# Turning one attention's operands through DRAM instead of on TensorE, in a two-block transformer kernel

## The chip, the cores and the metric

The kernel runs on one core of a Trainium2 chip. The metric is the device time of one execution in microseconds (us), lower is better. A difference is told as a share of the time before.

## What is computed

Two transformer blocks follow each other on 256 tokens of width 2048, all in f32. The first block:

```python
mod = silu(c) @ w_ada + b_ada
shift_a, scale_a, gate_a, shift_f, scale_f, gate_f = split(mod, 6)
h = rms_norm(x, g_attn_pre) * (1 + scale_a) + shift_a
proj = h @ w_in                     # d_q, d_k, d_v, s_q, s_k, s_v, i_q, i_k, i_w
diff = (softmax(q1 k1^T) - lam * softmax(q2 k2^T)) @ v    # 8 heads, causal
dsa  = attention over the 64 best keys of each query      # 8 heads, one shared key
mixed = concat(rms_norm(diff), dsa) @ w_o
x = x + gate_a * rms_norm(mixed, g_attn_post)
ff = (silu(h2 @ w_gate) * (h2 @ w_up)) @ w_down           # h2: x normed and modulated
x = x + gate_f * rms_norm(ff, g_ffn_post)
```

The second block projects the normed `x` by `w_in_2` (2048 to 19520 columns), has a latent attention (two latents of 512, `qa` and `ck`, each normed and projected up again), a gated convolution of length 3, two output products, a merge and `w_out_2`.

## The kernel before

**Products.** 256 tokens are two tiles of 128 (`t` = 0, 1). Each large product is a `Grp` of up to 512 output columns; it walks over the contraction in chunks of 128 rows (`kc`). Weights are f32; ScalarE (ACT) rounds a weight tile into `wh` and VectorE (DVE) computes the rest `wl` (`pump_split`, L286 and L287), two chunks at a time, and TensorE (PE) multiplies three times for each chunk and token tile: `hi*wh`, `hi*wl`, `lo*wh`. These are the rows `mm` of line L65. The left operand lies transposed, features on partitions, as a pair `hi`, `lo`.

**Order.** The program is written out once, in Python, in the order of a model clock: `run` issues the products one after the other and adds up PE's modelled time in `clock["t"]`; everything else is a generator in `bg` (softmax stages, norms, evictions) that yields how long it wants to be left alone, and `tick` resumes it when the model clock has come that far. So the model decides only in which order each engine's queue is filled; on the chip each queue runs in that order, as fast as its semaphores let it. Where a product needs something that the model has not finished, `require` resumes the generators one after the other with no product between them, and then `keep_warm` (L346) issues 12 dummy 512-column products before the real one.

**Buffers.** 14 slots of 1 MB (`big`, `free`) hold all large tensors. Weights are loaded by SP into a ring of 4 `raw` buffers; `lend(n)` adds up to n of the free slots to the ring (`rawb`).

**The first attention block.** The projection accumulates the columns of `w_in` in SBUF in slices: `accA0`, `accA1` (keys and queries of four difference heads each), `accS` (queries of the sparse attention), `accC`, `accV`. The last 12 chunks of the difference columns come in the order of `D_G`: 1024, 0, 2048 (first half: heads 0 to 3), 1536, 512, 2560 (second half). Merged into these products are those of the modulation rows (`ada`, 1 MB of `w_ada` for four narrow products). `idx_gen` scores and picks the keys, `dsa_gen` is the sparse attention, `diff_gen` the difference attention. Each attention is a `pipe` of stages: scores on PE (`sA`), softmax (`sB`, `sC`), transposed probabilities on PE (`sD`), product with the values (`sE`), norm (`sF`), transposed result (`sG`), which writes `mh0`, `ml0`. `diff_gen` runs two pipes, one for each half: it waits for `dsa`, ropes `accA`, turns four blocks of 128x512 by four PE transposes each (`quad_transpose`, L70), which ACT and DVE copy from PSUM into `kTz` and `dqT`, and starts the pipe of four heads for both token tiles. `w_o` comes in two products: `wo1` (needs the sparse attention, with `ada` rows merged in) and `wo2` (needs the difference attention, through `need=["diff", "ada2"]`).

**Other places.** `row_fin` spreads a modulated gate row over 128 partitions by four f32 products with a column of the identity (`br` and `brt`, L732). `lora_norm` turns a latent by `quad_transpose`; `post_ck1` turns the rope key `kd`; `post_z` turns group 0 of the gated attention.

**The way through DRAM** exists already as `flip_quad` (L558): DVE transposes 32x32 blocks into `scr`, four DMAs on SP write them to a DRAM tile in runs of 128 bytes, so that it lies transposed, and one DMA reads it back. It is used for the feed-forward activations and for most groups of the second block.

## Time and profile before

| | before |
|---|---|
| median of 3 runs | 2349.62 us (2348.67 to 2350.85) |
| profiled execution | 2349.08 us, its span 2347.4 us |
| PE busy | 2295.9 us, 98% of the span |
| DVE, ACT, POOL busy | 1331.7, 1066.2, 96.8 us |
| chain of work that ended last | 73% of the span on PE, 70% of it in `mm` of L65 |
| DMA | 528.60 MB, mean 225 GB/s |

Busy time of an engine is the union of its instructions' durations. Consecutive products overlap in the records: a 512-column `mm` lasts 0.39 us but the next starts 0.23 us later, so what a product costs is read from the distance of the starts.

### The profile page before, as it was taken

To read this page: it belongs to the slowest core of one execution; us is meant where nothing else is said; L and a number is where in the kernel's file an instruction comes from. 1 tells how busy PE (TensorE), PEld (TensorE's weight loads), DVE (VectorE), ACT (ScalarE), POOL (GpSimd) and SP (SyncE) were. 2 spreads that over 40 slices of the span, in tenths; PEclk is the share of its full clock that TensorE was granted. 3 is DMA by queue.
4 is the path that set the end of the run, shared out by engine and by line. 5 is a ranking of instruction groups with operands and counts; after the bars stand their busy time and mean duration, and the time that the engine had idled before them with its cause. 6 is when DMAs were issued, how large, how long until landed. Compare 5 with 4: busy or idle time off the path is not lost.

```text
span 2347.4 us, 27890 instructions
## 1 busy us (share of the span) xinstructions
PE 2295.9 (98%) x10876; PEld 1824.8 (78%) x10876; DVE 1331.7 (57%) x1752; ACT 1066.2 (45%) x1495; POOL 96.8 (4%) x117
## 2 busy tenths in 40 slices
PE   7899999999999999999998999999999999999998
PEld 5666666677887888888887888888888988888887
DVE  3646755556765455554556655656645654664665
ACT  4434344546444444434444644444445544444443
POOL 1311011010000000000001000000000000000000
PEclk9999999999999999999999999999999999999999
DMA  9987888868885566655764667776665553686773
GB/s 308 329 317 242 310 306 303 316 212 291 261 293 200 195 209 209 211 197 190 210 201 154 222 201 213 222 223 211 202 199 162 168 173 126 185 259 200 222 228 126
DMA packets 348500, 528.60 MB, mean 225 GB/s; under 512 B 98664, under 2 KB 142864, under 8 KB 339280
## 3 DMA queue, kind: packets, MB, share of 16 engines
q1 hardware_dynamic: 346272, 518.18, 67.6%
q0 software_dynamic: 1872, 8.58, 1.1%
q8 instruction: 85, 1.39, 0.2%
q14 instruction: 47, 0.39, 0.0%
q10 hardware_dynamic: 224, 0.07, 0.0%
HBM read 511.57 MB, written 15.20 MB: 224 GB/s over the span
## 4 chain that ended last, share of the span: by engine, by line
PE 73%; DVE 2%; ACT 1%; DMA 1%; issue 1%; SPq 0%; POOL 0%; DVEq 0%; POOLq 0%; ACTq 0%
PE mm L65 70%; PE sc L65 1%; PE tp L65 1%; DMA fm<-flip 1%; PE tp L70 1%; DVE wl L287 0%; SPq L566 0%; PE tpb L70 0%; ACT wh L286 0%; DVE xr L1175 0%; ACT h3h L1183 0%; DVE h3l L1186 0%; POOL rstd L513 0%; ACT junk L1198 0%; DVE ot L1740 0%
## 5 line engine op out<-in xcount | busy, mean ns | idle before, releaser
L287 DVE TENSOR_TENSOR wl<-raw,wh 128x1024 fp32r<-128x1024 f32 (+3 forms) x723 | 869.2, 1210 | 741.1 <-ACT wh L286 735.0
L286 ACT ACTIVATE wh<-raw 128x1024 fp32r<-128x1024 f32 (+3 forms) x723 | 745.7, 1039 | 736.4 <-PE mm L65 710.9
L65 PE MATMUL mm<-wh,h3h 128*128 128x512 f32 (+1 forms) x992 | 385.5, 389 | 1.7 <-ACT h3h L1183 1.2
L65 PE MATMUL mm<-wl,h3h 128*128 128x512 f32 (+1 forms) x992 | 380.9, 384 | 1.2 <-DVE wl L287 1.2
L65 PE MATMUL mm<-wh,h3l 128*128 128x512 f32 (+1 forms) x992 | 380.9, 384 | 0.0
L65 PE MATMUL mm<-wl,h2h 128*128 128x512 f32 x704 | 274.5, 390 | 0.9 <-DVE wl L287 0.9
L65 PE MATMUL mm<-wh,h2h 128*128 128x512 f32 x704 | 274.8, 390 | 0.0
L65 PE MATMUL mm<-wh,h2l 128*128 128x512 f32 x704 | 274.4, 390 | 0.0
L65 PEld LDWEIGHTS mm<-wh,h3h 128*128 128x128 f32 x992 | 186.8, 188 | 38.9 <-ACT h3h L1183 1.6
L65 PEld LDWEIGHTS mm<-wh,h3l 128*128 128x128 f32 x992 | 186.5, 188 | 37.3 <-DVE h3l L1186 0.4
L65 PEld LDWEIGHTS mm<-wl,h3h 128*128 128x128 f32 x992 | 186.8, 188 | 36.4 <-DVE wl L287 1.7
L65 PE MATMUL mm<-wh,h1h 128*128 128x512 f32 (+2 forms) x384 | 153.9, 401 | 3.9 <-ACT wh L286 3.1
L65 PEld LDWEIGHTS mm<-wl,h2h 128*128 128x128 f32 x704 | 132.6, 188 | 28.5 <-DVE wl L287 1.2
L65 PEld LDWEIGHTS mm<-wh,h2h 128*128 128x128 f32 x704 | 132.5, 188 | 28.3 <-issue 0.8
L65 PEld LDWEIGHTS mm<-wh,h2l 128*128 128x128 f32 x704 | 132.4, 188 | 27.3
L65 PE MATMUL mm<-wl,h1h 128*128 128x512 f32 (+2 forms) x384 | 142.7, 372 | 8.0 <-DVE wl L287 8.0
L65 PE MATMUL mm<-wh,h1l 128*128 128x512 f32 (+2 forms) x384 | 142.1, 370 | 1.9 <-DVE h1l L647 1.9
L65 PE MATMUL mm<-wh,acth 128*128 128x512 f32 x352 | 139.3, 396 | 0.0
L65 PE MATMUL mm<-wh,actl 128*128 128x512 f32 x352 | 137.1, 390 | 0.0
L65 PE MATMUL mm<-wl,acth 128*128 128x512 f32 x352 | 136.9, 389 | 0.0
L65 PEld LDWEIGHTS mm<-wh,h1h 128*128 128x128 f32 x384 | 72.7, 189 | 56.2 <-issue 25.9
L65 PEld LDWEIGHTS mm<-wl,h1h 128*128 128x128 f32 x384 | 73.0, 190 | 21.3 <-DVE wl L287 10.9
(413 smaller groups left out, 2753.1 us busy)
## 6 DMA issues: line engine op xcount, KB each, us to landing
raw<-in_w_in_dram SPq DMA_DIRECT2D x134, 1024.0 KB, 5.3
raw<-in_w_ada_dram SPq DMA_DIRECT2D x47, 1024.0 KB, 5.2
raw<-in_w_gate_dram SPq DMA_DIRECT2D x44, 1024.0 KB, 5.2
raw<-in_w_up_dram SPq DMA_DIRECT2D x44, 1024.0 KB, 5.5
raw<-in_w_down_dram SPq DMA_DIRECT2D x44, 1024.0 KB, 5.1
raw<-in_w_ada_dram SPq DMA_DIRECT2D x36, 512.0 KB, 8.4
rawb<-in_w_ada_dram SPq DMA_DIRECT2D x17, 1024.0 KB, 6.8
raw<-in_w_o_conv_dram SPq DMA_DIRECT2D x16, 1024.0 KB, 5.1
```

What stands on the lines that cost most here:

```text
L65: return nc.tensor.matmul(o, l, r, **kw)
L70: return nc.tensor.transpose(o, i, idn)
L286: A.activation(wh[:, :m, :g.n], src, AF.Copy)
L287: V.tensor_sub(wl[:, :m, :g.n], src, wh[:, :m, :g.n])
```

## The change

Three groups of edits. **First attention:** the operands of both attentions leave `accS` and `accA` through DRAM. `flip_quad` is split into `flip_out` (turn, write) and `flip_in` (read back); `dsa_prep` and the new `diff_out` issue these DMAs on POOL. The destination slots are asked for by `claim`, which waits until slots are free and keeps the ring from taking them. `diff_gen` starts after the last score product of the sparse attention (`dsascores`) instead of after its end, and runs one pipe over all 16 items; `ready` holds the whole pipe in front of an item whose operands have not been read back. **Rows:** `row_fin` writes the four pieces of a gate row to DRAM and reads them back on every partition. **Second block:** the two latents, `kd` and group 0 of `post_z` go through DRAM on SP's queue.

The diff, without its unchanged lines (the list of `diff_gen`'s second half is cut):

```diff
@@ -200 +200 @@
-    lent = {"now": 0, "max": 0}
+    lent = {"now": 0, "max": 0, "claims": 0}
@@ -215 +216 @@
+    def claim(n):
+        lent["claims"] += n
+        while True:
+            while len(slots) < n and reclaim():
+                pass
+            if len(slots) >= n:
+                break
+            yield POLL
+        lent["claims"] -= n
+
@@ -216 +227 @@
+        if it["res"][0] == "big" and len(slots) < lent["claims"]:
+            slots.append(it["res"][1])
+            lent["now"] -= 1
+            return
@@ -246 +260 @@
-                if lent["now"] < lent["max"] and len(slots) > 0:
+                if lent["now"] < lent["max"] and len(slots) > lent["claims"]:
@@ -366 +380 @@
-    def pipe(items, stages, offs, every):
+    def pipe(items, stages, offs, every, ready=None):
@@ -372 +387 @@
+            if ready is not None and j == 0:
+                while not ready(items[i]):
+                    yield POLL
@@ -558 +575 @@
-    def flip_quad(src, dst=None):
+    def flip_out(src, n=512, wait=2.0, scr=None, eng=nc.sync):
@@ -561 +578 @@
-        scr = wtile(tag="PT", bufs=2, name="scr")
-        V.transpose(scr, src)
-        yield 2.0
+        if scr is None:
+            scr = wtile(tag="PT", bufs=2, name="scr")
+        v = scr[:, :n]
+        V.transpose(v if len(src.shape) == 2 else v.rearrange("p (h d) -> p h d", h=src.shape[1]), src)
+        yield wait
@@ -565 +584 @@
-            d = bass.AP(tensor=dr.tensor, offset=dr.offset + 32 * i, ap=[[P, 32], [32 * P, 16], [1, 32]])
-            nc.sync.dma_start(d, scr[32 * i:32 * i + 32].rearrange("p (b r) -> p b r", r=32))
+            d = bass.AP(tensor=dr.tensor, offset=dr.offset + 32 * i, ap=[[P, 32], [32 * P, n // 32], [1, 32]])
+            eng.dma_start(d, scr[32 * i:32 * i + 32, :n].rearrange("p (b r) -> p b r", r=32))
@@ -567 +587 @@
+        return dr
+
+    def flip_in(dr, dst, b0=0, step=4, p0=0, n=P, eng=nc.sync):
+        s = bass.AP(tensor=dr.tensor, offset=dr.offset + b0 * 32 * P + p0 * P,
+                    ap=[[P, n], [step * 32 * P, dst.shape[1]], [1, P]])
+        eng.dma_start(dst, s)
+
+    def flip_quad(src, dst=None):
+        dr = yield from flip_out(src)
@@ -570 +598 @@
-        s = bass.AP(tensor=dr.tensor, offset=dr.offset, ap=[[P, P], [P * P, 4], [1, P]])
-        nc.sync.dma_start(dst, s)
+        flip_in(dr, dst)
@@ -730 +757 @@
-            for j in range(4):
-                pb = tp_bank()
-                T.matmul(pb, ident[:, 32 * j:32 * j + 1].to_broadcast([P, P]), br, start=True, stop=True)
-                A.activation(hid[name][:, 512 * j:512 * (j + 1)], pb, AF.Copy)
-                yield
+            line = drp.tile([4, 512], F32, name=f"line{name}")
+            G.dma_start(line, br[0:P:32, :])
+            yield 10.0
+            G.dma_start(hid[name], bass.AP(tensor=line.tensor, offset=line.offset, ap=[[0, P], [1, D]]))
+            yield 10.0
@@ -872 +900 @@
+        mark("picks")
@@ -902 +930 @@
-        sqT = big("sqT")
-        hid["sqT"] = sqT
+        drs = {}
@@ -909 +936 @@
-                pb = quad_transpose(acc["S"][:, t, 512 * q:512 * (q + 1)])
-                A.activation(sqT[:, 4 * q:4 * q + 4, t * P:(t + 1) * P], pb, AF.Copy)
-                yield 2.07
+                drs[t, q] = yield from flip_out(acc["S"][:, t, 512 * q:512 * (q + 1)], eng=G)
@@ -915 +941 @@
+        while not done("picks"):
+            yield POLL
+        yield from claim(1)
+        sqT = big("sqT")
+        hid["sqT"] = sqT
+        for t in range(2):
+            for q in range(2):
+                flip_in(drs[t, q], sqT[:, 4 * q:4 * q + 4, t * P:(t + 1) * P], eng=G)
+        yield FLIP
@@ -936 +971 @@
+            if it == (1, 3):
+                mark("dsascores")
@@ -980 +1017 @@
+    kTz = {}
+
+    def diff_out(q):
+        while not done(f"win{512 * q}_d.1", f"win{1024 + 512 * q}_d.1"):
+            yield POLL
+        src = acc["A", q]
+        for t in range(2):
+            rope(src[:, t].rearrange("p s (n d) -> p (s n) d", d=64)[:, :, 0:16], 16, t)
+        yield 4.0
+        drs = {}
+        for t in range(2):
+            for s in range(2):
+                drs[t, s] = yield from flip_out(src[:, t, 1 - s, :], 512, 3.0, wtile(name="scr"), G)
+        free(f"accA{q}")
+        while not done("dsa" if q else "dsascores"):
+            yield POLL
+        yield from claim(1 if q else 2)
+        if q == 0:
+            hid["dqT"] = big("dqT")
+        dqT = hid["dqT"]
+        kTz[q] = big(f"kTz{q}", (P, 4, 2, 256))
+        G.memset(kTz[q], 0.0)
+        yield 4.0
+        for t in range(2):
+            tok = slice(t * P, (t + 1) * P)
+            flip_in(drs[t, 0], kTz[q][0:64, :, 0, tok], 0, 4, 0, 64, G)
+            flip_in(drs[t, 0], kTz[q][64:128, :, 1, tok], 0, 4, 64, 64, G)
+            flip_in(drs[t, 1], dqT[:, 4 * q:4 * q + 4, tok], eng=G)
+        yield FLIP
+
@@ -982 +1048 @@
-        while not done("dsa"):
+        while not done("dsascores", "diffin0"):
@@ -984 +1050 @@
-        kTz = {}
-        dqT = big("dqT")
+        dqT = hid["dqT"]
@@ -1059 +1125 @@
+            mh, ml = mhml
@@ -1065 +1131 @@
-        for q in range(2):
-            kTz[q] = big(f"kTz{q}", (P, 4, 2, 256))
-            G.memset(kTz[q], 0.0)
...
-                pb = quad_transpose(src[:, t, 0, :])
-                A.activation(dqT[:, 4 * q:4 * q + 4, t * P:(t + 1) * P], pb, AF.Copy)
...
+        mhml = []
+
+        def ready(it):
+            q = it[1] // 4
+            if not done(f"diffin{q}", f"win{2048 + 512 * q}_d.1"):
+                return False
+            return bool(mhml)
+
+        def outputs():
+            while not done("dsa"):
@@ -1088 +1142 @@
-            yield from pipe([(t, h) for t in range(2) for h in range(4 * q, 4 * q + 4)],
-                            [sA, sB, sC, sD, sE, sF, sG],
-                            [0.0, 1.12, 4.01, 9.5, 12.09, 13.2, 19.98], 2.64)
-            free(f"kTz{q}")
+            yield from claim(2)
+            hid["mh0"], hid["ml0"] = big("mh0", dt=R32), big("ml0", dt=R32)
+            mhml.extend((hid["mh0"], hid["ml0"]))
+
+        spawn(outputs())
+        yield from pipe([(t, h) for q in range(2) for t in range(2) for h in range(4 * q, 4 * q + 4)],
+                        [sA, sB, sC, sD, sE, sF, sG],
+                        [0.0, 1.12, 4.01, 9.5, 12.09, 13.2, 19.98], 2.64, ready)
+        free("kTz0", "kTz1")
@@ -1110 +1170 @@
+    def start_out():
+        for q in range(2):
+            spawn(diff_out(q), f"diffin{q}")
+
@@ -1132 +1196 @@
+    sd.insert(0, call(start_out))
+    sd.insert(1, call(lambda: lend(2)))
@@ -1367 +1432 @@
-        yield
-        pb = quad_transpose(x)
-        m = wtile(name="lm")
-        m3 = m.rearrange("p (c q) -> p c q", q=P)
-        V.tensor_mul(m3, pb, col2[:, goff:goff + 4][:, :, None].to_broadcast([P, 4, P]))
+        go = flip_quad(x)
+        d = next(go)
+        mark(f"turned{goff}.{t}")
+        yield d
+        m3 = yield from go
+        V.tensor_mul(m3, m3, col2[:, goff:goff + 4][:, :, None].to_broadcast([P, 4, P]))
@@ -1387 +1453 @@
-        require([f"r3.{t}", "qa.0", "qa.1"], "ck0")
+        require([f"r3.{t}", "turned0.0", "turned0.1"], "ck0")
@@ -1402 +1468 @@
-        yield
-        pb = quad_transpose(kd[:, :P])
-        A.activation(zk[0:64, 0, t * P:(t + 1) * P], pb[0:64, 0, :], AF.Copy)
-        A.activation(zk[64:128, 1, t * P:(t + 1) * P], pb[64:128, 0, :], AF.Copy)
+        dr = yield from flip_out(kd[:, :P], P)
+        flip_in(dr, zk[0:64, 0:1, t * P:(t + 1) * P], 0, 4, 0, 64)
+        flip_in(dr, zk[64:128, 1:2, t * P:(t + 1) * P], 0, 4, 64, 64)
+        yield FLIP
@@ -1654 +1720 @@
-            if g:
-                m3 = yield from flip_quad(d)
-            else:
-                yield
-                m3 = quad_transpose(d)
+            m3 = yield from flip_quad(d)
```

How the rows of the queues move, at three places. In these rows `tp` is a PSUM bank for transposes and small products, `osb` the attention's output before it is turned, `p` the probabilities, `pt` the same transposed, `mh1`/`ml1` and `mh0`/`ml0` the operands of `wo1` and `wo2`, `adasb` the copy of a finished modulation row.

**PE, where `wo1` ends and `wo2` begins.** Before, the last row of the difference attention is the `osb` row here, and six products of `wo1`, an `ada` row of four products, six more products and another `ada` row lie between it and `wo2`:

```order
L65 MATMUL mm_4094<-wh_4030,mh1_2607 128x512
L65 MATMUL mm_4094<-wl_4031,mh1_2607 128x512
L65 MATMUL mm_4094<-wh_4030,ml1_2608 128x512
L70 MATMUL tp_4159<-ident_99,osb_4092 128x128 x4
L65 MATMUL mm_4076<-wh_4070,mh1_2607 128x512
L65 MATMUL mm_4076<-wl_4071,mh1_2607 128x512
L65 MATMUL mm_4076<-wh_4070,ml1_2608 128x512
```

After the change, at the end of `wo1`:

```order
L65 MATMUL mm_3965<-wh_4028,ml1_2650 128x512
L65 MATMUL ada_3556<-raw_3861,csil_117 32x512 x4
L70 MATMUL tp_4168<-ident_99,p_4044 128x128 x2
L70 MATMUL tp_4172<-ident_99,osb_4095 128x128 x4
L70 MATMUL tp_4179<-ident_99,p_4081 128x128 x2
L70 MATMUL tp_4183<-ident_99,adasb_4155 128x128 x4
L65 MATMUL tp_4191<-accV_267,pt_4097 128x128 x4
L65 MATMUL tp_4191<-accV_267,pt_4167 128x128 x4
L70 MATMUL tp_4214<-ident_99,osb_4200 128x128 x4
L360 LDWEIGHTS negi_104
L360 MATMUL mm_4221<-caus_106,negi_104 128x512
```

The end of the difference attention now stands behind the last product of `wo1` with no large product between its rows, and the 12 dummy products of `keep_warm` (now L360) follow before `wo2`. The last score product of the difference attention stands 78 large products ahead of `wo2` before and 18 after the change. The first half's scores hardly move; the second half's first score product stands 66 products later than before, and ahead of it the pipe of all 16 items issues nothing on PE for 156 large products.

**ACT, at the same place.** Before, from the last copies of the difference attention on:

```order
L1022 ACTIVATE pt<-tp 128x256
L286 ACTIVATE wh<-raw 128x1024
L1037 ACTIVATE osb<-tp 128x512
L1046 ACTIVATE sq<-osb 128x512
L286 ACTIVATE wh<-raw 128x1024 x2
L1061 ACTIVATE mh_3151<-tp,gdiff 128x4x128
```

After the change:

```order
L1223 ACTIVATE mo_3523<-mm 128x512
L726 ACTIVATE adasb<-ada 128x512
L300 ACTIVATE wh<-rawb 128x1024 x2
L1087 ACTIVATE pt<-tp 128x256
L1127 ACTIVATE mh_3151<-tp,gdiff 128x4x128
L1087 ACTIVATE pt<-tp 128x256
L1102 ACTIVATE osb<-tp 128x512
L1111 ACTIVATE sq<-osb 128x512
L1127 ACTIVATE mh_3151<-tp,gdiff 128x4x128
```

The copy of the modulation row and two weight splits now stand ahead of the last two `pt` copies.

**POOL, from the first half's end to the second half's scores.** Before:

```order
L800 TENSOR_TENSOR accA_266<-pa,accA_266 128x512
L513 TENSOR_TENSOR rstd<-rstdv,mhalf 128x4
L800 TENSOR_TENSOR accV<-pa,accV 128x512
L513 TENSOR_TENSOR rstd<-rstdv,mhalf 128x4
L1067 MEMSET kTz_3612 128x2048
```

After:

```order
L585 DMA flip_3535<-scr 32x16x32 x4
L760 DMA Ga<-lineGa 128x2048
L585 DMA flip_3632<-scr 32x16x32 x4
L1038 MEMSET kTz_3708 128x2048
L592 DMA kTz_3708<-flip_3317 64x4x128 x2
L592 DMA dqT<-flip_3440 128x4x128
L592 DMA kTz_3708<-flip_3535 64x4x128 x2
L592 DMA dqT<-flip_3632 128x4x128
L530 TENSOR_TENSOR rstd<-rstdv,mhalf 128x4 x3
```

Each half now has 16 writes and 6 reads on POOL's queue, behind the additions into `accA` and around the clearing of `kTz`.

## Rows read from the trace of the kernel before

**Rows 1.** Windows: window, length, busy us of PE, PEld, DVE, ACT, POOL, clock, DMA share, GB/s.

```profile
240.00:480.00 240.00, 240.00 (x1225) 148.82 (x1224) 147.34 (x327) 110.23 (x232) 21.98 (x22) 1.00 0.86 313
```

**Rows 2.** Timeline of PE: start, length, engine, line, operation, out<-in, shape, count.

```profile
411.94 1.02 PE L65 MATMUL tp<-br,ident 128*128 128x512 f32 x2
412.40 0.79 PE L65 MATMUL mm<-wh,mh 128*128 128x512 f32 x1
413.03 0.39 PE L65 MATMUL mm<-wl,mh 128*128 128x512 f32 x1
413.26 0.40 PE L65 MATMUL mm<-wh,ml 128*128 128x512 f32 x1
...
418.97 0.60 PE L70 MATMUL tp<-ident,accA 128*128 128x128 f32 x4
419.32 0.47 PE L65 MATMUL mm<-wh,mh 128*128 128x512 f32 x1
419.64 0.39 PE L65 MATMUL mm<-wl,mh 128*128 128x512 f32 x1
419.86 0.39 PE L65 MATMUL mm<-wh,ml 128*128 128x512 f32 x1
```

**Rows 3.** Groups by line and shape: the dummy products of `keep_warm`; DVE's block transposes.

```profile
L346 PE MATMUL mm<-caus,negi 128*128 128x512 bf16 x24 | 5.5, 379 | 0.0
...
L562 DVE STREAM_TRANSPOSE scr<-act 128x512 f32<-128x512 f32 x16 | 11.4, 711 | 0.6
```

**Rows 4.** Timeline of all engines: the last heads' way from `pt` to `osb`.

```profile
463.04 0.39 ACT L1022 ACTIVATE pt<-tp 128x256 f32<-128x256 f32 x1
...
465.01 1.95 PE L65 MATMUL tp<-accV,pt 128*128 128x128 f32 x16
...
467.00 0.60 ACT L1037 ACTIVATE osb<-tp 128x512 f32<-128x512 f32 x1 [2.63 <-PE tp L65]
467.62 0.63 ACT L1046 ACTIVATE sq<-osb 128x512 f32<-128x512 f32 x1
...
469.26 1.01 POOL L513 TENSOR_TENSOR rstd<-rstdv,mhalf 128x4 f32<-128x4 f32 x1 [10.85 <-DVE rstdv L511]
...
470.30 0.88 DVE L1051 TENSOR_SCALAR osb<-osb,rstd 128x128 f32<-128x128 f32 x4 [1.12 <-POOL rstd L513]
...
472.25 1.06 PE L65 MATMUL ada<-raw,csil 128*32 128x512 f32 x8
472.35 1.06 ACT L286 ACTIVATE wh<-raw 128x1024 fp32r<-128x1024 f32 x1 [2.90 <-PE mm L65]
...
476.10 0.60 PE L70 MATMUL tp<-ident,osb 128*128 128x128 f32 x4
476.73 0.69 ACT L1061 ACTIVATE mh<-tp,gdiff 128x512 fp32r<-128x512 f32 x1 [3.32 <-PE tp L70]
```

**Rows 5.** Timeline of PE at a wait later in the kernel.

```profile
1284.74 1.12 PE L70 MATMUL tp<-ident,xr 128*128 128x128 f32 x4 [4.72 <-DVE xr L1175]
```

**Rows 6.** Windows around that wait.

```profile
1280.00:1284.00 4.00, 0.02 (x1) 0.00 (x0) 2.61 (x7) 2.96 (x7) 0.54 (x1) 0.94 0.00 0
1284.00:1290.00 6.00, 5.26 (x19) 4.57 (x20) 5.04 (x7) 2.33 (x7) 0.00 (x0) 0.50 0.33 98
1290.00:1296.00 6.00, 5.60 (x29) 4.39 (x28) 3.94 (x6) 3.25 (x9) 0.00 (x0) 0.97 0.00 0
```

**Rows 7.** Windows of 50 us without a way through DRAM, and with two.

```profile
800.00:850.00 50.00, 50.00 (x222) 41.40 (x222) 22.59 (x19) 21.38 (x23) 0.00 (x0) 1.00 0.60 190
850.00:900.00 50.00, 50.00 (x222) 41.42 (x221) 25.90 (x25) 22.29 (x23) 0.00 (x0) 1.00 0.69 212
```

**Rows 8.** POOL's own: a DMA's time on the engine, and the clearing of `kTz`.

```profile
L456 POOL DMA_DIRECT2D pos<-in_positions_dram x2: 727/743/759, 26.8 to 27.6; - x2
...
344.85 1.81 POOL L1067 MEMSET kTz<- 128x2048 f32 x1 [3.04 <-PE tp L65]
```

**Rows 9.** The page's DMA issues: queue, count, size, median us to landing.

```profile
raw<-in_w_o_dram SPq DMA_DIRECT2D x11, 1024.0 KB, 7.0
...
br<-in_b_ada_dram POOLq DMA_DIRECT2D x4, 64.0 KB, 7.3
```

More of the change, by code (lines that the diff above doesn't have):

```diff
@@ L1063, in sG @@
                                    op1=OP.subtract)
-        for q in range(2):
-            kTz[q] = big(f"kTz{q}", (P, 4, 2, 256))
-            G.memset(kTz[q], 0.0)
-            while not done(f"win{512 * q}_d.1", f"win{1024 + 512 * q}_d.1"):
-                yield POLL
-            src = acc["A", q]
-            for t in range(2):
-                rope(src[:, t].rearrange("p s (n d) -> p (s n) d", d=64)[:, :, 0:16], 16, t)
-            yield 7.0
-            for t in range(2):
-                pb = quad_transpose(src[:, t, 1, :])
-                A.activation(kTz[q][0:64, :, 0, t * P:(t + 1) * P], pb[0:64], AF.Copy)
-                V.tensor_copy(kTz[q][64:128, :, 1, t * P:(t + 1) * P], pb[64:128])
-                yield 1.89
-                pb = quad_transpose(src[:, t, 0, :])
-                A.activation(dqT[:, 4 * q:4 * q + 4, t * P:(t + 1) * P], pb, AF.Copy)
-                yield 1.89
-            free(f"accA{q}")
-            if q == 0:
-                mh, ml = big("mh0", dt=R32), big("ml0", dt=R32)
-                hid["mh0"], hid["ml0"] = mh, ml
-            while not done(f"win{2048 + 512 * q}_d.1"):
-                yield POLL
-            yield from pipe([(t, h) for t in range(2) for h in range(4 * q, 4 * q + 4)],
-                            [sA, sB, sC, sD, sE, sF, sG],
-                            [0.0, 1.12, 4.01, 9.5, 12.09, 13.2, 19.98], 2.64)
-            free(f"kTz{q}")
+        mhml = []
[6 more added lines that the diff above has]
+            while not done("dsa"):
+                yield POLL
+            yield from claim(2)
[6 more added lines that the diff above has]
+        free("kTz0", "kTz1")
         set_state("sc_free", True)
```

## The prediction

> **What bounds the kernel now.** I read the page first, then windows of 50 us: PE is busy 98% of the span, and from 240 to 480 us, the stretch that holds both attentions and the first product with `w_o`, all of it: 240.00 of 240.00 us [rows 1]. No other engine is near that there (DVE 147, ACT 110 us), so in this stretch a saving counts only where it takes work from PE, and every wait of PE that the change makes is paid in full. The DMA engines are the second resource to watch: 0.86 of 240 us, 206 us [rows 1]. The sum below is made against the profiled execution, 2349.08 us, which is 0.5 us under the median of the three runs. A measurement of this kernel can tell about 0.2% from no change, 4.7 us.
>
> **What PE is rid of.** A group's busy time counts the overlap with the next product, so I read what a piece costs from the starts. The 512-column products follow each other 0.23 us apart (413.03 to 413.26). One gate-row product and three `mm` rows: from 411.94 to 413.26 there lie the row product and two `mm`, 1.32 us, less two times 0.23: 0.86 us [rows 2]. Four transposes (a quad) and two `mm`: 418.97 to 419.86 is 0.89 us, less 0.46: 0.43 us [rows 2]. The change takes away 8 row products (6.9 us), the quads of `accA` (8), `accS` (4), the latents (4) and group 0 of `post_z` (2), together 18 quads (7.7 us), and two single transposes of `kd` (some 0.3 us): **-14.9 us** of PE time. Nothing else on PE leaves, apart from the order.
>
> **What replaces it, off PE.** Sixteen DVE block transposes of 128x512 at 0.71 us [rows 3], in place of evictions from PSUM on ACT and DVE: free, as long as DVE stays as far from full as now (147 of 240 us). The second block's new ways through DRAM run on SP's queue like those already there, in stretches where PE is full and DMA is at 0.6 to 0.7 [rows 7]; each has a whole group of products or more before its reader. I cost them at nothing; without that cover each would cost PE a wait of a few us. The `Ga` and `Gf` rows are read long after they are written.
>
> **Where `wo2` waits: the main new cost.** `wo2` needs the whole difference attention. Before, the last score product stands 78 large products ahead of it, and the last `osb` row has two half-units of `wo1` behind it; the trace shows no wait. After, the second half starts later and only 18 large products lie behind the last score product. I follow the tail by hand, from the end of that score product (0). PE has 18 `mm` (4.1 us), two `ada` rows at 1.0 (2.0), four f32 products with the values (half of the 1.95-us row, 0.9) and two pairs of transposes (0.5): it reaches the end of `wo1` at 7.5. ACT then has, in this order, the copy of the modulation row (0.6), two weight splits (1.06 each), a `pt` (0.39), an `mh` (0.69) and the last `pt` (0.39) [rows 4]: with the semaphores between them it is done at 12.2, and only then the eight products with the values can start. From their start to the end of the norm's scaling the trace has 465.01 to 471.18, 6.2 us [rows 4], through ACT, DVE, POOL and DVE again. So the last `osb` quad starts at about 18.5. Of the 11.0 us since 7.5 PE has work for 3.1 (two pairs, two quads, the value products at 1.7, their 1.95 less the overlap): **+7.9 us** idle. Bounds: 5.8, if the two splits are done before the copies are wanted (2.1 us less), and 10, if POOL or DVE come 2 us late. Then come 12 dummy products, 5.5 us for 24 [rows 3], so **+2.8 us**. The copy into `mh` (0.69) and the rest of it are hidden behind the dummies.
>
> **The clock after it.** At 1284.74 PE had sat idle for 4.72 us [rows 5]; around there the granted clock fell, and from 1284 to 1290 it stood at 0.50, the lower of the two levels (1.2 of 2.4 GHz), while PE was busy for 5.26 us [rows 6]. Half of that, 2.6 us, is what the fall cost. The longest idle piece that I forecast is from the end of the value products (14.1) to 18.5, 4.4 us, near to that row, so I take the full price, **+2.7 us**; bounds 0 and 2.7.
>
> **The first score product of each half.** It now waits for `kTz` and `dqT` from DRAM. In the first half POOL has the second addition into `accA`, the clearing (1.81 us), three reads to issue (0.74 us each, the nearest row: 256 single runs) and a landing of 7.3 us for the nearest POOL row [rows 8, 9], some 13 us with the addition; 54 large products (12.4 us), three `ada` rows and some attention rows, some 17 us, stand between. The second half has some 20 us between the last block transpose and the score product, for 14.3 (four writes, clearing, three reads, landing). Both fit. Bounds 0 and 5; I take **+1.0 us**. The sparse attention's `sqT` has the whole choice of keys as cover.
>
> **DMA.** Two ways through DRAM raise the share of a 50-us window from 0.60 to 0.69 [rows 7]: 2.2 us of all engines each. Eight whole ones, four reads (half of one each) and the 1-MB row are 17.6 + 4.4 + about 3: 25 us on top of 206, in some 240. That is 0.96, full but not over; the ring of four to six buffers must carry the unevenness. Bounds 0 and 7 (one landing of a weight tile, 7.0 us [rows 9]); I take **+1.0 us**, near the lower end, because PE has not waited for a weight there so far [rows 1].
>
> **The sum.** -14.9 + 7.9 + 2.8 + 2.7 + 1.0 + 1.0 = +0.5: **2349.6 us**, the gain given back at one place.
>
> **Rivals.** *The gain is kept.* If ACT has the two splits behind it when the copies are wanted, and the idle time in three pieces does not bring the clock down: -14.9 + 5.8 + 2.8 = -6.3, 2342.8 us. For it: in the trace ACT is busy for less than half of this stretch [rows 1]; against it: the order puts these splits behind the copy of a row that PE finishes only at 7.5. Chance 0.27. *POOL's DMAs are late (slower).* Before, POOL never issued a DMA of 512 short runs; 0.74 us is the row for 256 [rows 8]. The second half's cover is gone when each DMA takes POOL about 1.5 us (6 + 1.8 + 4.5 + 7.3 = 19.6 of 20). At four times the row, 3 us, the first half comes 3 us late and the second 10, and the wait at `wo2` stays: 2361.6 us. For it: 44 of these DMAs for the two halves, in a queue that had next to none; against it: POOL issues 32-row and 256-run DMAs at nearly the same price. The Trainium skill, SBUF — State Buffer, section "SBUF: two separate sides", says that while DVE runs certain copies with one input in SBUF, GpSimd is locked out of the shared port and cannot write descriptors, so its DMAs look blocked, and advises SP's or ACT's queue. No run so far shows it; it would make each issue at most one short DVE instruction longer (0.88 us for four [rows 4], so 0.2 us each), which stays under the point of 1.5 us. Chance 0.18. *Weights come late.* The DMA share goes to 1 in parts and PE waits for one landing more: 2355.6 us, chance 0.13. *The one pipe is no one pipe:* that is so already in the order (nothing from it for 156 large products) and is part of the forecast.
>
> **How the numbers follow.** The forecast has 0.42 (its own range 2345 to 2354). Faster by over 0.2% is the first rival, 0.27; the same is the forecast, 0.42; slower are the other two, 0.31. The range, 2342 to 2361, reaches to the first rival's and nearly to the second's time and leaves out the tails of both.
>
> **What would show it.** Right: PE idle for 6 to 10 us behind the last product of `wo1`, ended by the scaling of `osb` and by `pt`; dummies at the new line; a granted clock near 0.5 just behind; the groups `accA`, `accS`, `br`, `brt` gone; no wait for `kTz` or `dqT` over 3 us. Wrong: no such wait (then 2343), a wait of PE in front of the score products or for `wl` between 240 and 480 us (then 2355 and more), or a wait in the second block, which I cost at nothing.

## The result and the profile after

The changed kernel takes 2367.07 us (median of 4 runs, 2363.08 to 2369.76); the kernel before, run beside it, 2350.23 us (4 runs). The ratio is 1.007, with a 95% interval of 1.0059 to 1.0082: **slower, by 16.8 us**, where 2349.6 us was forecast. The profiled execution took 2365.61 us, its span is 2363.9 us.

Two rows tell where the loss lies. The first product of `wo1` and the last of `wo2` are the first and last start of the group `mm<-wh,mh`, in the kernel before:

```profile
L65 PE MATMUL mm<-wh,mh x128: 389/389/792, 399.6 to 525.0; 128*128 128x512 f32 x128
```

and in the changed one:

```profile
L65 PE MATMUL mm<-wh,mh x128: 389/389/795, 396.5 to 541.4; 128*128 128x512 f32 x128
```

`wo1` starts 3.1 us earlier: eight quads are gone ahead of it, and one quad of the first half's `osb`, which stood ahead of it before, now stands behind. `wo2` ends 16.4 us later: 19.5 us are lost in between. Behind it the distance stays between 13.8 and 17.6 us, and the span ends 16.5 us later. Windows of the changed kernel over this stretch (busy time of PE, PEld, DVE, ACT and POOL, clock, DMA share, GB/s; [rows 1] had PE busy all through at clock 1.00):

```profile
400.00:410.00 10.00, 10.00 (x58) 6.18 (x50) 3.41 (x6) 2.62 (x3) 1.79 (x3) 1.00 1.02 405
410.00:420.00 10.00, 10.00 (x54) 5.87 (x54) 2.82 (x3) 2.61 (x3) 7.65 (x10) 1.00 1.02 400
420.00:430.00 10.00, 8.64 (x48) 4.66 (x40) 0.06 (x1) 0.00 (x0) 0.76 (x1) 1.00 1.05 317
430.00:440.00 10.00, 8.05 (x30) 4.92 (x31) 3.62 (x4) 4.98 (x6) 0.00 (x0) 0.83 1.02 410
440.00:450.00 10.00, 10.00 (x55) 6.23 (x54) 5.26 (x15) 3.82 (x12) 0.00 (x0) 1.00 1.02 404
450.00:460.00 10.00, 10.00 (x63) 6.41 (x62) 5.65 (x17) 5.11 (x15) 1.05 (x1) 1.00 1.03 403
460.00:470.00 10.00, 9.38 (x43) 5.51 (x44) 7.11 (x21) 4.28 (x12) 0.00 (x0) 1.00 0.69 240
470.00:480.00 10.00, 8.54 (x52) 4.97 (x50) 6.52 (x20) 8.31 (x20) 1.01 (x1) 1.00 0.34 114
480.00:490.00 10.00, 5.37 (x22) 4.41 (x22) 5.39 (x12) 3.75 (x7) 0.00 (x0) 0.66 0.32 114
490.00:500.00 10.00, 7.50 (x23) 4.06 (x24) 2.47 (x7) 0.69 (x1) 2.10 (x3) 0.66 0.55 211
```

There are two holes. The small one is at 425 to 440 us. Ahead of it, from 420 to 430 us, DVE and ACT do nothing, because ACT waits for weights to land (ACT's waits for transfers in 396 to 460 us: total, times, longest):

```profile
ACT wh L300 <- DMA raw<-in_w_o_dram: 20.3, 3, 11.5
ACT wh L300 <- DMA rawb<-in_w_o_dram: 7.3, 1, 7.3
```

The large one, 470 to 500 us, is the gate of `wo2`, its wait for `diff`. PE's timeline there (in brackets the idle time ahead of a row and the row that ended it):

```profile
478.73 0.60 PE L70 MATMUL tp<-ident,osb 128*128 128x128 f32 x4
482.22 0.66 PE L70 MATMUL tp<-ident,p 128*128 128x128 f32 x2 [2.89 <-ACT mh L1127]
483.36 1.11 PE L70 MATMUL tp<-ident,adasb 128*128 128x128 f32 x4 [0.47 <-ACT pt L1087]
485.06 3.60 PE L65 MATMUL tp<-accV,pt 128*128 128x128 f32 x16 [0.59 <-DVE ml L1128]
492.50 1.08 PE L70 MATMUL tp<-ident,osb 128*128 128x128 f32 x4 [3.84 <-DVE osb L1116]
493.37 5.33 PE L360 MATMUL mm<-caus,negi 128*128 128x512 bf16 x12
498.14 0.80 PE L65 MATMUL mm<-wh,mh 128*128 128x512 f32 x1
```

The idle pieces are 2.89 + 0.47 + 0.59 + 3.84 = 7.8 us. What runs between them runs at about half speed: the value products take 3.60 us (1.95 in [rows 4]), the last quad 1.08 (0.60 in [rows 4]), the 12 dummies 4.77 from their start to that of the product behind them (2.75 by [rows 3]).

### The profile page after: what moved, and what is told of

Read it like the earlier page. It is cut to its first block, busy times and chain, and to the rows that moved or that the text cites. A ratio compares the mean times of both kernels' runs of the same rounds, so it can differ in the third digit from the quotient of the medians.

```text
span 2363.9 us, 27885 instructions
## 1 busy us (share of the span) xinstructions
PE 2295.6 (97%) x10798; PEld 1821.0 (77%) x10798; DVE 1337.8 (57%) x1768; ACT 1052.9 (45%) x1471; POOL 140.3 (6%) x185
## 4 chain that ended last, share of the span: by engine, by line
PE 74%; DVE 2%; ACT 1%; DMA 1%; issue 1%; SPq 0%; POOL 0%; DVEq 0%; POOLq 0%; ACTq 0%
PE mm L65 71%; DMA fm<-flip 1%; PE tp L65 1%; PE sc L65 1%; DVE wl L301 1%; PE tp L70 1%; ACT wh L300 0%; PE tpb L70 0%; SPq L585 0%; POOL rstd L530 0%; DMA raw<-in_w_gate_dram 0%; PE mm L360 0%; PE ada L65 0%; DVE xr L1240 0%; ACT p L925 0%
```

## The experiments

Theory H: the loss is the lateness of the second half, made by the plan (four flips one after the other at 3 + 8 us of plan each, and one pipe that stands still meanwhile). Rival T: the loss is the added DRAM traffic, which keeps weights back. Medians are told as the distance to the kernel before, run beside each.

**1. The operands 3 us apart.** In `diff_out`:

```diff
-                drs[t, s] = yield from flip_out(src[:, t, 1 - s, :], 512, 3.0, wtile(name="scr"), G)
+                spawn(one(t, s))
+                yield 3.0
+        while len(drs) < 4:
+            yield POLL
```

> The four operands of the second half leave accA1 three us of plan apart instead of eleven, so that its first score product stands 1233 large products into the program and not 1302, and its last quad of outputs 24 products ahead of wo2 and not behind its gate. Theory H (the one pipe, held until those operands are in, is the loss): the stretch without attention shrinks from 156 to 87 products, the 7.8 us idle at the gate of wo2, the 5.3 us of the dummies and the half clock at 480 to 498 go: 2367 - 19 = 2344 to 2350 us. Rival T (the added DRAM traffic of the operands and of Ga is the loss, since it keeps weights back): the traffic is the same and stands closer together, so TensorE's waits at 425 to 440 us stay or grow and the half clock behind them with them: 2355 to 2362 us.

Measured: 2356.78 us (+6.8; ratio 1.0028, 1.0017 to 1.0038). The gate is open in time, with no dummies at it and no half clock at 480 to 500. But the wait for weights has grown. Window of PE (busy, clock, DMA share, GB/s):

```profile
410.00:420.00 10.00, 4.05 (x20) 0.85 1.02 383
```

and PE's two longest waits in 400 to 460 us:

```profile
PE mm L65 <- ACT wh L300: 5.5, 1, 5.5
PE tp L65 <- ACT pt L1094: 3.0, 1, 3.0
```

The time lies where T had it and the gate as H had it: opening the gate in time is worth 10 us even with the longer wait for weights, and that wait is real. The second wait, inside the attention at 450 us, neither theory had.

**2. A pipe that holds back only what isn't ready**, alone:

```diff
-            if ready is not None and j == 0:
-                while not ready(items[i]):
-                    yield POLL
-            stages[-j](items[i])
+            elif ready is not None and not ready(items[n]):
+                due = t + POLL
+            else:
+                stages[0](items[n])
+                ev += [(t + offs[j], -j, n) for j in range(1, len(stages))]
```

> The pipe of the change holds back only the heads that are not ready; the operands leave accA1 as slowly as before. The first half's stages end at 1200 products instead of 1344, but the second half's scores still begin at 1296 (1302 in the change), and its last quad still stands behind the gate of wo2. Theory H, with the lateness of the second half as its price: the idle time at the gate, the dummies and the half clock behind them stay (about 15 us), the wait for weights at 425 to 440 gets shorter by up to half of its 3 us and of the half clock around it: 2361 to 2366 us. A form of H in which the blocked first half is the price: 2350 to 2356 us. Rival T: no change, 2364 to 2369 us.

Measured: 2362.27 us (+12.3; 1.0045, 1.003 to 1.0059). As H has it with the lateness as the price: idle pieces of 2.65 and 3.34 us and the dummies are still there.

**3. Both edits, of runs 1 and 2.**

> As the run with the operands 3 us apart, and beside that a pipe that holds back only the heads that are not ready and lets those already begun go on. The first half's last stages then stand at 1140 to 1176 products and the second half's last quad 36 products ahead of wo2. Theory H: no more than the early start alone gives, since no wait is left at the gate: 2342 to 2349 us, within 3 us of that run. Rival T: 2355 to 2362 us, as there.

Measured: 2350.19 us (+0.2; 1.0002, 0.9993 to 1.0012). Both holes are gone, and with the same traffic as in run 1 no wait for weights is left. H missed here: it had at most 3 us beside run 1, and this is 6.6 us faster, since the wait for weights went with the hold. Of the 17 us this gives back all, but a gain it is not, though PE has 14.9 us less to do than in the kernel before, by the prediction's count. Its waits in 300 to 530 us (the first lies behind `wo2` and is 2.2 us in the kernel before):

```profile
PE tp L65 <- DVE dg L1281: 2.1, 1, 2.1
PE tp L70 <- ACT osb L1117: 2.0, 2, 1.6
PE mm L65 <- ACT pa L834: 1.5, 1, 1.5
PE sc L65 <- ACT p L933: 1.0, 1, 1.0
PE sc L65 <- issue: 0.6, 1, 0.6
```

**4. The order of the change without the traffic of the second half's operands and of `Ga`.**

```diff
+            if which == 2:
+                G.memset(hid[name], 1.0)
+                yield 20.0
+                return
...
-                drs[t, s] = yield from flip_out(src[:, t, 1 - s, :], 512, 3.0, wtile(name="scr"), G)
+                if q == 0:
+                    drs[t, s] = yield from flip_out(src[:, t, 1 - s, :], 512, 3.0, wtile(name="scr"), G)
+                else:
+                    V.transpose(wtile(name="scr"), src[:, t, 1 - s, :])
+                    yield 3.0
+                    yield FLIP
...
-        for t in range(2):
+        if q:
+            G.memset(dqT[:, 4:8, :], 0.0)
+        for t in range(2 if q == 0 else 0):
```

> The order on TensorE is that of the change, row for row, and so is the hold. Left out: the second half's operands are neither written to DRAM nor read back (its kTz and its half of dqT are filled with zeros on GpSimd at the same place of the order), and Ga is filled with ones in place of its line and its broadcast; some 3 MB less in flight between 390 and 450 us. Theory H: the loss stays at the gate of wo2 (idle 7 to 9 us, dummies 5, half clock) and most of the wait for weights stays too: 2360 to 2367 us. Rival T: the waits for weights at 425 to 440 go, and the time falls to 2350 to 2356 us.

Measured: 2364.33 us (+14.4; 1.0058, 1.0043 to 1.0073). PE's windows: the small hole is gone, the large one is as it was.

```profile
420.00:430.00 10.00, 10.00 (x54) 1.00 1.02 411
430.00:440.00 10.00, 10.00 (x52) 1.00 1.02 406
...
470.00:480.00 10.00, 5.41 (x36) 0.95 0.60 212
480.00:490.00 10.00, 6.11 (x24) 0.50 0.15 38
```

The wait for weights went as T had it, the time stayed as H had it. So traffic makes the wait for weights, but that is only some 2.7 us of the medians (2367.07 to 2364.33), which the two intervals don't tell from nothing. Runs 3 and 4 together, with one profile each: it needs both, the traffic and a stretch in which PE has nothing but weights to use up.

**5. The lateness alone, on the kernel before.** One line ahead of its second pipe:

```diff
             while not done(f"win{2048 + 512 * q}_d.1"):
                 yield POLL
+            if q:
+                yield 18.0
```

> The kernel before, all operands turned on TensorE, nothing through DRAM that was not there; one yield of 18 us of plan ahead of the second half's pipe puts its first score product at 1302 large products, where the change has it (before: 1236), and its last quad behind the gate of wo2. Theory H: the lateness alone makes the loss: idle 7 to 8 us at the gate, 12 dummies of 5 us, half clock behind: 2362 to 2368 us. Rival T (traffic) and any theory that needs the operands' way through DRAM: 2350 to 2353 us.

Measured: 2365.38 us (+15.6; 1.0068, 1.0054 to 1.0081). PE's timeline at its gate is much that of the change, with 6.4 us idle in four pieces, the longest of them here:

```profile
484.88 3.62 PE L65 MATMUL tp<-accV,pt 128*128 128x128 f32 x16
492.28 1.03 PE L70 MATMUL tp<-ident,osb 128*128 128x128 f32 x4 [3.77 <-DVE osb L1051]
493.10 4.16 PE L346 MATMUL mm<-caus,negi 128*128 128x512 bf16 x12
```

No operand of the first attention went through DRAM here. In this profile 14.1 us are lost between the first product of `wo1` and the last of `wo2`. The lateness by 66 products is enough for a loss of this size: for the gate, H is shown.

**6. The change without the dummies.**

```diff
-                    keep_warm(g, ts[0])
+                    if not g.name.startswith("wo2"):
+                        keep_warm(g, ts[0])
```

> The change without the 12 dummy products that are recorded when wo2's gate isn't open in the plan; all else as it was. If the dummies cost what they take (theory D1, 5.3 us at half clock in the profile of the change): 2361 to 2363 us. If the products behind them pay for the clock in their place (theory D2, the engine is as long at half clock without them): 2365 to 2368 us, no difference that can be told.

Measured: 2364.46 us (+14.7; 1.0066, 1.005 to 1.0081), four runs from 2360 to 2369. Inconclusive: the median lies between the two forecasts and can't be told from the change. In its profile the first products of `wo2` run at the lower clock in place of the dummies (0.57 in 490 to 500 us).

**7. The rows alone, on the kernel before.** The change's edit of `row_fin`:

```diff
-            for j in range(4):
...
+            G.dma_start(line, br[0:P:32, :])
+            yield 10.0
+            G.dma_start(hid[name], bass.AP(tensor=line.tensor, offset=line.offset, ap=[[0, P], [1, D]]))
```

> The kernel before with Ga and Gf sent through DRAM and nothing else of the change. TensorE loses eight row products, 6.9 us. The attention stays spread as it was, so no theory of the hold applies. If the broadcasts are free: 2342 to 2344 us. If a broadcast of 1 MB at 400 to 412 us pushes the weights (theory T): each costs up to its 2.6 us of all transfers' time, so 2344 to 2348 us.

Measured: 2343.30 us (**-6.8**; 0.9971, 0.996 to 0.9982). PE's work is given back whole; the broadcasts cost nothing that can be seen.

**8. The second block's part alone, on the kernel before.** The change's edits of `lora_norm`, `post_ck0`, `post_ck1` and `post_z`:

```diff
-        pb = quad_transpose(x)
+        go = flip_quad(x)
...
-        pb = quad_transpose(kd[:, :P])
+        dr = yield from flip_out(kd[:, :P], P)
...
-            if g:
-                m3 = yield from flip_quad(d)
-            else:
-                yield
-                m3 = quad_transpose(d)
+            m3 = yield from flip_quad(d)
```

> The kernel before with the second block's part of the change alone: the two latent quads, kd and the first quad of each at go through DRAM instead of TensorE, the first attention and the rows stay as they were. TensorE's work falls by 2.4 us. If those turned operands arrive in time (theory P, as forecast): 2347 to 2349 us. If they are the cause of the 2 to 6 us that the last stage (from the last product on att to the last on merh) lost in every variant so far, and of the half us lost at the latents (theory S): 2351 to 2357 us, with the last stage 2 us or more longer than before's 88.6.

Measured: 2353.83 us (+3.8; 1.0016, 1.0006 to 1.0025): as theory S, and not as forecast. The last stage takes 90.9 us in its profile, 88.6 in that of the kernel before.

**9 and 10. The second block turned on PE again, in run 3's kernel; and with `Ga` broadcast later.** Both take back the edits of run 8; run 10 adds to `row_fin`:

```diff
             yield 10.0
+            while which == 2 and not done("wo1_2.0"):
+                yield POLL
             G.dma_start(hid[name], bass.AP(tensor=line.tensor, offset=line.offset, ap=[[0, P], [1, D]]))
```

> The early operands and the pipe that lets begun heads go on, with the latents, kd and the first quad of at turned on TensorE as before. Theory S (the second block's part loses the last stage): the last stage is back at 88.6 us, and the time is 2350.2 - 5 = 2343 to 2346 us. Rival R (the last stage is lost by what the first attention left behind: other slots lent to the ring of weights): the last stage stays at 93 to 95 us, and the time at 2350 to 2353 us.

> As the kernel beside it (early operands, pipe that lets begun heads go on, second block as before), and the 1 MB broadcast of Ga is issued only when the third quarter of wo1 is done, at about 462 us instead of 403 us, when the transfers have room. If the added traffic in 400 to 460 us still keeps weights back (theory T, now for what is left: 3.4 us of idle TensorE in 400 to 450): 1.5 to 3 us faster than the kernel beside it. If not: the same within 1 us.

Measured: 2346.68 us (-3.4; 0.9986, 0.9976 to 0.9995) and 2348.88 us (-1.2; 0.9992, 0.9983 to 1.0001). Against run 3 the first gives back 3.5 us, nearly the amount of run 8 from the other side. But its profile still has 3.7 us of wait for `thm` and 93.4 us in the last stage, as R had it, while the time is nearer to S. By the medians the price belongs to the second block's part; by this profile it is not the last stage that gives it back. Run 10 fits neither of its forecasts: the later broadcast gains nothing.

**11 and 12. Less of the first attention through DRAM.** Run 11: rows and `accS` only (`diff_gen` as before). Run 12: rows, `accS` and the first half's `accA`, the second half's turned on PE, run 2's pipe, second block as before. In `diff_out` of run 12:

```diff
+            if q == 0:
...
+            else:
+                pb = quad_transpose(src[:, t, 1, :])
+                A.activation(kTz[q][0:64, :, 0, tok], pb[0:64], AF.Copy)
+                V.tensor_copy(kTz[q][64:128, :, 1, tok], pb[64:128])
+                yield 1.89
+                pb = quad_transpose(src[:, t, 0, :])
+                A.activation(dqT[:, 4 * q:4 * q + 4, tok], pb, AF.Copy)
```

> The kernel before with Ga and Gf through DRAM and with the sparse attention's queries (four quads of accS, 1.7 us of TensorE) through DRAM too; the dense attention and the second block as before. If a part turned through DRAM in good time gives its work back: 2343.3 - 1.7 = 2341 to 2342.5 us. If the first score product waits for what is read back, as a 1.5 us wait at 340 to 380 us in the runs with early operands suggests: 2343 to 2345 us.

> The rows, accS and the first half's accA through DRAM, the second half's accA turned on TensorE, the pipe that lets begun heads go on, the second block as before. TensorE's work is 6.9 + 5.1 - 1.7 = 10.3 us less than before's; the second half's scores stand at 1176 products (before: 1236), the last quad 72 products ahead of wo2. Theory H alone: 2340 to 2343 us. If what was left of the loss in the runs with early operands (about 3.5 us of idle TensorE between 360 and 450 us) came from the first half's way through DRAM: 2343 to 2347 us; if from the second half's: 2340 to 2343 us.

Measured: 2342.41 us (**-7.4**; 0.9966, 0.9953 to 0.9978) and 2351.79 us (+2.0; 1.0006, 0.9997 to 1.0015). Run 11 cannot be told from run 7. Run 12 is slower than both of its forecasts, though its last quad stands 72 products ahead of `wo2`: in this form, with the one pipe, the first half's way through DRAM doesn't pay even when nothing is late at the gate. Its largest wait of PE in 300 to 480 us is a new one:

```profile
PE tp L70 <- DVE kTz L1059: 2.6, 2, 2.5
```

**13 and 14. The second block's two parts, each alone on the kernel before.** Run 13: the edits of run 8 for the latents and `kd`. Run 14: the one of `post_z`, for the first quad of `at`.

> The kernel before with the two latents' four quads and kd through DRAM, the first quad of at turned on TensorE as before. TensorE's work is 2.0 us less. Theory P (forecast): 2347.5 to 2348.5 us. If the latents are what made the second block's part 3.8 us slower (theory L: what reads the turned latents, or the clock behind a short wait at 1324 to 1334 us, gives back more than the work): 2351 to 2354 us.

> The kernel before with the first quad of each at through DRAM and nothing else. TensorE's work is 0.9 us less. Theory P (forecast): 2348.5 to 2349.5 us. If this part is what made the second block's part slower (theory A: the last stage, from the last product on att to the last on merh, gets longer than before's 88.6 us by the wait of the transposes of thm): 2351 to 2354 us.

Measured: 2354.09 us (+4.1; 1.0010, 1.0000 to 1.0019) and 2350.82 us (+0.8; 1.0000, 0.9991 to 1.0009). The median of run 13 lies further off than its ratio, since its eleven executions lie in two groups, 2349.1 to 2350.7 and 2352.7 to 2354.9. Neither part gains, and by the medians the loss is with the latents. There, PE's windows (busy, clock, DMA share, GB/s) and its wait for DVE's part of a weight's split, `wl`, in 1270 to 1420 us, first of the kernel before:

```profile
1310.00:1320.00 10.00, 10.00 (x78) 1.00 0.60 173
1320.00:1330.00 10.00, 9.58 (x72) 1.00 0.89 299
PE mm L65 <- DVE wl L287: 0.4, 1, 0.4
```

then of run 13:

```profile
1310.00:1320.00 10.00, 8.26 (x56) 0.90 0.58 189
1320.00:1330.00 10.00, 10.00 (x73) 0.93 1.04 276
PE mm L65 <- DVE wl L287: 1.7, 1, 1.7
```

PE is idle for 1.74 us instead of 0.42, up to 1316.71, and the clock at 0.90 and 0.93 takes another 1.7 us of the 20: some 3.0 us lost for 2.0 us of work saved. From the first product on `h3h` to the first on `yh` it is 410.5 us, 410.1 in the kernel before, so by the starts 2.4 us are lost.

This wait isn't for a transfer: ACT, which splits first, waits for none in 1300 to 1322 us. The split stands late in DVE's queue. In the kernel before, from the first row of the latents' norm to the split:

```profile
1308.80 0.49 DVE L1383 TENSOR_SCALAR qa<-qa,r 128x512 f32<-128x512 f32 x1 [0.51 <-ACT qa L1378]
...
1313.87 1.42 DVE L287 TENSOR_TENSOR wl<-raw,wh 128x576 fp32r<-128x576 f32 x2
```

In run 13 two block transposes lie in between, of which this is the second:

```profile
1309.39 0.49 DVE L1394 TENSOR_SCALAR qa<-qa,r 128x512 f32<-128x512 f32 x1 [0.52 <-ACT qa L1389]
...
1315.30 0.71 DVE L564 STREAM_TRANSPOSE scr<-qa 128x512 f32<-128x512 f32 x1
1315.93 2.72 DVE L287 TENSOR_TENSOR wl<-raw,wh 128x576 fp32r<-128x576 f32 x4
```

The split comes 6.5 us behind that first row, not 5.1. No run moved it ahead of the transposes. PE's wait of 1.7 us at this place is in the profiles of all eight kernels that turn the latents through DRAM (the change and runs 1 to 4, 6, 8 and 13). The fall of the clock behind it is in three of them (the change, runs 8 and 13), and there the stretch takes 410.5 to 410.6 us; in the other five the clock stays at 1.00 and the stretch takes 409.0 to 409.5 us.

The rest of this execution's loss (2354.84 us) lies for the most part in the last stage. From the last product on `att` to the last on `merh` it takes 92.9 us, 88.6 in the kernel before, with a wait of PE for `thm` of 3.1 us there:

```profile
PE tp L70 <- DVE thm L1707: 3.1, 1, 3.1
```

That wait was 0.4 us in the kernel before, 0.6 in run 14, 1.8 in run 7 and up to 5.1 in run 4; the stage takes 88.6 us in the kernel before and 88.8 to 94.7 in all others, also in those that have it in common with the kernel before. So one profile of the kernel before told too little of it. In the traces the `thm` rows stand on DVE behind rows that wait for ACT, and ACT waits for `fm<-flip` to land, a way through DRAM that the kernel before has too: for 3.7 us there, 6.3 in run 13 and 7.0 in run 4. What makes that landing late is open; no run tried it.

## Why the prediction was wrong

The parts, measured alone on the kernel before, nearly add up: rows -6.8, second block +3.8, lateness of the second half +15.6, together +12.6 of +16.8; 4.2 us are left for the rest of the first attention. Runs 9 and 7, with the gate open, give nearly the same for it: -3.4 against -6.8 us, +3.4. These are differences of medians, and each holds its own share of the last stage, which differs by up to 6 us between profiles. Against the steps of the prediction:

| step | forecast | shown |
|---|---|---|
| the eight row products | -6.9 | -6.8 (run 7) |
| the gate of `wo2`: idle, dummies, clock | +13.4 | +15.6 (run 5) |
| the second block: 6 quads and `kd` | -2.9 | +3.8 (run 8) |
| the first attention's 12 quads, first scores, weights | -3.2 | +4.2 (what is left) |

**The gate was read right, and a little too cheap.** The idle time was forecast as 7.9 us and is 7.8, with the releasers named (`osb`'s scaling, `pt`, and ACT's `mh` ahead of it, bound up with the two splits). The step that was mis-sized is *The clock after it*: 2.7 us, from a stretch where PE was idle in one piece. Here the clock fell earlier, within the tail. Value products, quads and dummies already ran at about half speed: 1.65 + 2.0 + 1.0 = 4.7 us. With 7.8 idle and 2.75 for the dummies at full speed that is 15.2 us where 13.4 was forecast; run 5 measured 15.6.

**The second block, "I cost them at nothing", is the first step that failed**, and with it the block transposes called free "as long as DVE stays as far from full as now". The cover that the prediction asked for was there: in run 13 PE waits for no turned operand between `h3h` and `yh`. But a block transpose is not free where a weight's split stands behind it in DVE's queue, and a mean share (147 of 240 us, far from the latents) doesn't tell that: two of them made the split 1.5 us later, PE waited for it, and in the change the clock fell behind the wait. Of the 2.0 us saved at the latents none came through in the change and 0.6 to 1.1 us in five other profiles. That explains a part of the 6.7 us between -2.9 and +3.8; in the profiles of runs 8 and 13 another 2.3 and 4.3 us lie in the last stage, and whether the latents' way has to do with them stays open. (The prediction's "sixteen" block transposes are eighteen in the diff.)

**"-14.9 us of PE time" counted the first attention's 12 quads as gained. That is the second step that failed.** The rows show 3.1 us gained up to the start of `wo1`, part of it work moved behind. But then weights come late (PE idle 2.6 + 0.8 us, clock 0.83 for 10 us). The step *DMA*, "full but not over", had a mean of 0.96; the windows from 400 to 460 show 1.02 to 1.05. In 396 to 460 us SP's queue moved 22.4 MB (20.1 before) and POOL's another 2.6: that fits a held stretch in which PE uses up weights faster, since the second half's attention is still to come. The price by run 4 is 2.7 us, within the bounds of 0 to 7, not told from nothing by its interval. What remains isn't settled: with the gate open and no wait for weights (runs 3, 9, 12), waits between the attention's stages add up to 5.1, 4.4 and 2.9 us in the profiles, about what the quads save there (5.2, 5.2 and 3.4).

**The first score products** were cheaper than the 1.0 us put in for them: PE waits for neither `kTz` nor `dqT` in the changed kernel. **The rival *POOL's DMAs are late* fell**: four writes took POOL 2.63 us, 0.66 each, and a read 0.63 to 0.77, under the point of 1.5. The timeline of POOL, four writes and the last read:

```profile
390.50 2.63 POOL L585 DMA_DIRECT2D flip<-scr  x4
...
420.15 0.76 POOL L592 DMA_DIRECT2D dqT<-flip  x1 [0.72 <-DMA flip<-scr]
```

The Trainium skill, SBUF — State Buffer, section "SBUF: two separate sides", lets POOL's DMAs look blocked behind certain DVE copies; no issue here shows that. The last read of the second half was issued by 420.9 us, the two of its kind in 396 to 460 us landed 8.8 us after their issue in the median, and the first score product that needs it started at 443.2, by this estimate some 13 us after the landing: the 156 products without attention are the plan's, not the transfers'. That "the one pipe is no one pipe" was named and its effect on the gate was counted; its effect on the use of weights was not. *Weights come late* (2355.6 us) had the right wait at the wrong size, and alone.

The version to keep is run 7 or run 11: 2343.3 and 2342.4 us, both faster than the kernel before and some 24 us faster than the change, not told apart.

## What to carry to other kernels

Where a plan sets the order of queues, look at what the plan believes a wait costs: four transfers planned one after the other made the second half 66 products late, though the operands were there some 13 us sooner. Work that one engine loses must be asked for stretch by stretch: PE was rid of 14.9 us, but only the 6.9 us without a wait nearby came through. A row given to an engine with time to spare still delays what stands behind it in that queue, here a weight's split by 1.5 us. And here work that uses no weights was what let the weights' transfers keep up with PE; taken out of a stretch or moved behind, the same traffic that was hidden became a wait.

## What was not expected of the hardware

With the transfers' share at 1.0, the time from issue to landing of a 1-MB weight tile rose. In the changed kernel, 396 to 460 us (the last figure is the median in us):

```profile
raw<-in_w_ada_dram SPq DMA_DIRECT2D x7, 1024.0 KB, 13.2
raw<-in_w_o_dram SPq DMA_DIRECT2D x4, 1024.0 KB, 16.5
```

In the kernel before, 400 to 460 us, with a share of 0.72 to 1.00 in windows of 10 us:

```profile
raw<-in_w_ada_dram SPq DMA_DIRECT2D x7, 1024.0 KB, 5.0
raw<-in_w_o_dram SPq DMA_DIRECT2D x3, 1024.0 KB, 5.2
```

The tiles that went into lent slots (`rawb`) took 9.7 and 14.8 us, 6.8 in the kernel before. A share at 1.0 alone did no harm: in run 4 it is 1.02 to 1.04 from 400 to 440 us, the weight tiles land in 6.9 to 10.3 us (medians of four groups, 396 to 460 us), and PE is never idle there. Twelve dummies that were meant to keep the clock up ran at the lower clock themselves in the change (4.77 us), and taking them away moved the time by less than can be told.
